# The inverse root of the norm of x: eight VectorE steps against one power on GpSimd

## The chip, the cores and the metric

The kernel runs on one core of a Trainium2 chip. Its time is the device time of one execution in microseconds (us). Five engines take part, each with an instruction queue of its own that it works off in order: TensorE (PE, with PEld for its weight loads), VectorE (DVE), ScalarE (ACT), GpSimd (POOL) and SyncE (SP, which here issues most of the transfers). An engine waits for another by a semaphore, and whatever stands behind a waiting instruction in the same queue waits with it.

## The reference, cut to what matters

Two blocks follow each other on 256 tokens of width 1024: a mixer block of two layers with a mixture of experts in each, and one attention block. Every stage begins with the same root-mean-square norm of x:

```python
def rms_norm(x, gain):
    xf = x.astype(jnp.float32)
    y = xf * lax.rsqrt(jnp.mean(xf * xf, axis=-1, keepdims=True) + EPS)
    return (y * gain.astype(jnp.float32)).astype(x.dtype)

for l in range(DEPTH):                      # DEPTH = 2
    h = rms_norm(x, attn_norm[l])
    proj = h @ w_in[l]
    ...                                     # matrix LSTM, attention, spatial gating
    x = x + y @ w_out[l]
    x = x + hier_moe(rms_norm(x, ffn_norm[l]), ...)
...
h = rms_norm_2(x, norm_w[l])                # the second block, once
proj = h @ w_in_2
```

That makes five norms of x: two at a mixer, two at a router of the experts, one at the second block. What the change touches is the `rsqrt` in these five, for 256 tokens, which lie as 128 partitions by 2 columns.

## The kernel before, in words

The 256 tokens are two tiles of 128 rows. The projections stream weights of 1 MB (`w`, five buffers, issued by SP in `pump`, line 188), and each chunk is split into two parts of reduced precision, `whi` by ScalarE (line 263) and `wlo` by VectorE (line 264). Every product is then three matmuls (lines 452, 453, 454) over eight slices of 128 channels. The experts' weights stream in the same way, unsplit.

The norm isn't applied to x before the product. `transpose_x` transposes the raw x, TensorE starts on the product at once, and the factor `rx` (one number for each token) comes in afterwards. `norm` (line 408) forms it: line 411 adds the two half sums of squares and EPS, and `rsqrt` (lines 334 to 341) takes an integer guess and eight VectorE steps to the inverse root. Who needs `rx`:

- In a mixer, `rh` (lines 504 and 505, VectorE) and `across` (line 426): TensorE spreads `rx` over the partitions with small matmuls, VectorE copies the result to `rb` (line 429). `across` stands in TensorE's queue amid the matmuls of the first projection.
- In a router, the scaled logits `lg` (line 953, VectorE). They head a chain of some twenty small VectorE steps up to `ab` (line 975), which TensorE needs for its next real work (line 977). Ahead of that it does 22 matmuls that serve nothing but to keep it busy (`warm(22)`, line 392).
- In the second block, `across` alone, and later the scales of the projections.

GpSimd does little: the rotary tables times a gain (lines 520 and 521, sixteen short products in each layer, from the table `row`, whose transfer line 291 issues), the mask of `wst` (line 698), `rg` (line 701) and some fills. In layer 1 `row` is loaded from ScalarE's queue when the layer begins.

The order on each engine is not the order of the source. The framework that builds the program sets it ahead of time from estimates of its own, and the engines then keep to it.

Of the kernel before, what the change touches and what calls it, by code (L numbers as in the profile page):

```python
# [15 lines left out]
OP = mybir.AluOpType  # L16
# [91 lines left out]
def block_kernel(ctx: ExitStack, tc: tile.TileContext, A, out):  # L108
    nc = tc.nc
# [41 lines left out]
    def small(shape, dt=F32, name="t", bufs=1):  # L151
        return sp.tile(shape, dt, name=name, tag=shared.get(name, name), bufs=bufs)
# [174 lines left out]
    def rsqrt(v):  # L327

        n = v.shape[1]
        c = (3.0 / 8) ** 0.2
        y, t = small([128, 24], name="rs_y", bufs=2)[:, :n], small([128, 24], name="rs_t", bufs=2)[:, :n]
        nc.vector.tensor_scalar(y.bitcast(I32), v.bitcast(I32), -0.5, 1597463007.0, op0=OP.mult, op1=OP.add)
        nc.vector.scalar_tensor_tensor(t, y, -0.5 * c, y, op0=OP.mult, op1=OP.mult)
        nc.vector.tensor_mul(t, t, v)
        nc.vector.scalar_tensor_tensor(y, t, 1.5 * c, y, op0=OP.add, op1=OP.mult)
        nc.vector.tensor_mul(t, y, y)
        nc.vector.tensor_mul(t, t, v)
        nc.vector.scalar_tensor_tensor(t, t, -2.251600503921509, t, op0=OP.add, op1=OP.mult)  # L340
        nc.vector.scalar_tensor_tensor(v, t, 2.2813665866851807, y, op0=OP.add, op1=OP.mult)
# [66 lines left out]
    def norm(s4):  # L408

        r = small([128, 2], name="rx", bufs=2)  # L410
        nc.vector.scalar_tensor_tensor(r, s4[:, :, 0], EPS, s4[:, :, 1], op0=OP.add, op1=OP.add)
        rsqrt(r)
        return r

    def norm_stats():
        s4 = small([128, 2, 2], name="ss4")
        for n in range(2):
            for j in range(2):
                square(s4, j, n)
        return norm(s4)  # L420
# [482 lines left out]
    class Router:  # L903
# [35 lines left out]
        def route(self):  # L939
            l, xh, xl, pt = self.l, self.xh, self.xl, self.pl  # L940
            R = row[l]
            warm(22)
            r = norm(self.s4)
            rh, r2 = small([128, 2], name="r_h"), small([128, 2], name="r_2")
            nc.gpsimd.tensor_scalar(rh, r, 0.5, None, op0=OP.mult)
# [727 lines left out]
```

## Time and profile before

| what | value |
|---|---|
| three timed runs | 964.05, 967.74, 968.22 us (median 967.74) |
| the profiled execution | 964.06 us, its span 962.3 us |
| TensorE busy (matmul) | 935.0 us, 97% of the span |
| TensorE weight loads | 617.4 us, 64% |
| VectorE busy | 473.9 us, 49% |
| ScalarE busy | 378.3 us, 39% |
| GpSimd busy | 18.3 us, 2% |
| HBM read | 271.27 MB, 285 GB/s over the span |

The 964.06 us of the profiled execution are 1.8 us more than its span, which runs from the first to the last instruction. The four executions stand at two levels, near 964 and near 968 us. TensorE is busy nearly throughout, and its busy time counts pipelined matmuls whose ends are modelled, so what matters are the places at which it waits. The layers begin near 5 and 374 us, their routers stand near 145 and 506 us, and the second block begins near 735 us.

### The profile page before, as it was taken

The numbers are of one execution on the slowest core, as the hardware profiler recorded it, in microseconds if no ns is written. First come the engines' busy times: TensorE is split into PE (matmuls) and PEld (weight loads), VectorE is DVE, ScalarE is ACT, GpSimd is POOL, SyncE is SP. The second block draws the span as 40 slices with busy tenths as digits, with TensorE's granted clock in tenths as the row PEclk, the third lists the DMA queues.
The fourth block names the chain that finished last, engine by engine and source line by source line (L and its number), as shares of the span: only waits on it lengthen the run. The fifth ranks groups of instructions, "written<-read, shape, count | busy, mean of one in ns | idle before, by whom it ended". The sixth has DMA issues, their size and how long they took to land. (4 is left out here: it accounts for less than half of the span.)

```text
span 962.3 us, 14955 instructions
## 1 busy us (share of the span) xinstructions
PE 935.0 (97%) x5818; PEld 617.4 (64%) x5818; DVE 473.9 (49%) x1131; ACT 378.3 (39%) x706; POOL 18.3 (2%) x60
## 2 busy tenths in 40 slices
PE   8989999999999998999999999999998999999998
PEld 6889884433344345889884433344345988899996
DVE  5698765221111225788665221111225777786574
ACT  5576542212122124485532212122124446745442
POOL 0100000000000001100000000000000000000000
PEclk8999999999999999999999999999999999999999
DMA  9537558899999998347558899999998542155531
GB/s 356 182 131 304 189 217 325 333 401 422 420 423 419 412 421 343 103 147 291 184 220 331 325 407 422 421 421 418 421 421 350 182 163 94 45 176 178 187 118 44
DMA packets 41436, 273.36 MB, mean 284 GB/s; under 512 B 5128, under 2 KB 7312, under 8 KB 9872
## 3 DMA queue, kind: packets, MB, share of 16 engines
q1 hardware_dynamic: 39008, 268.48, 71.0%
q10 hardware_dynamic: 2352, 3.87, 1.3%
q8 instruction: 48, 0.79, 0.3%
q14 instruction: 28, 0.23, 0.1%
HBM read 271.27 MB, written 2.63 MB: 285 GB/s over the span
## 5 line engine op out<-in xcount | busy, mean ns | idle before, releaser
L1128 PE MATMUL mm<-w,X 128*32 128x512 f32 (+1 forms) x1024 | 188.8, 598 | 1.8 <-DMA w<-in_w_e 1.8
L264 DVE TENSOR_TENSOR wlo<-w,whi 128x1024 fp32r<-128x1024 f32 (+3 forms) x124 | 145.2, 1182 | 26.8 <-ACT whi L263 26.7
L263 ACT ACTIVATE whi<-w 128x1024 fp32r<-128x1024 f32 (+3 forms) x124 | 122.5, 1017 | 76.4 <-issue 42.4
L1167 PE MATMUL mm<-w,ehT 128*32 128x512 f32 (+1 forms) x512 | 136.0, 600 | 3.9 <-DMA w<-in_w_e 1.5
L452 PE MATMUL mm<-hT,whi 128*128 128x256 f32 (+2 forms) x432 | 124.9, 290 | 0.2
L454 PE MATMUL mm<-hT,wlo 128*128 128x256 f32 (+2 forms) x432 | 124.1, 287 | 0.8 <-DVE wlo L264 0.8
L453 PE MATMUL mm<-lT,whi 128*128 128x256 f32 (+2 forms) x432 | 124.1, 288 | 0.0
L1128 PEld LDWEIGHTS mm<-w,X 128*32 128x32 f32 (+1 forms) x1024 | 47.8, 119 | 93.7 <-issue 83.0
L453 PE MATMUL mm<-wlo,hT 128*128 128x256 f32 x288 | 83.3, 289 | 1.1 <-DVE wlo L264 1.1
L452 PE MATMUL mm<-whi,hT 128*128 128x256 f32 x288 | 84.2, 292 | 0.0
L454 PE MATMUL mm<-whi,lT 128*128 128x256 f32 x288 | 83.2, 289 | 0.0
L452 PEld LDWEIGHTS mm<-hT,whi 128*128 128x128 f32 (+2 forms) x432 | 80.3, 186 | 2.3 <-issue 0.8
L453 PEld LDWEIGHTS mm<-lT,whi 128*128 128x128 f32 (+2 forms) x432 | 80.2, 186 | 1.8 <-issue 1.3
L454 PEld LDWEIGHTS mm<-hT,wlo 128*128 128x128 f32 (+2 forms) x432 | 80.2, 186 | 1.6 <-DVE wlo L264 1.3
L1115 ACT ACTIVATE X<-mm,vec 128x256 f32<-128x256 f32 (+1 forms) x96 | 43.4, 456 | 94.6 <-PE mm L1112 93.8
L1171 DVE TENSOR_TENSOR yhl<-mm,yhl 128x512 fp32r<-128x512 f32 x44 | 30.4, 692 | 95.2 <-ACT yhl L1170 93.2
L1167 PEld LDWEIGHTS mm<-w,ehT 128*32 128x32 f32 (+1 forms) x512 | 32.6, 119 | 68.2 <-issue 54.9
L1112 PEld LDWEIGHTS mm<-P,xh 128*128 128x128 f32 x192 | 29.2, 188 | 49.2 <-ACT X L1115 32.5
L1153 DVE TENSOR_SCALAR ePT<-mm,C 128x256 fp32r<-128x256 f32 x22 | 10.7, 484 | 100.4 <-ACT ehT L1151 100.4
L453 PEld LDWEIGHTS mm<-wlo,hT 128*128 128x128 f32 x288 | 55.0, 191 | 2.9 <-DVE wlo L264 1.5
L452 PEld LDWEIGHTS mm<-whi,hT 128*128 128x128 f32 x288 | 55.0, 191 | 1.4 <-issue 0.7
L454 PEld LDWEIGHTS mm<-whi,lT 128*128 128x128 f32 x288 | 55.0, 191 | 0.7 <-issue 0.2
(456 smaller groups left out, 1387.6 us busy)
## 6 DMA issues: line engine op xcount, KB each, us to landing
w<-in_w_e SPq DMA_DIRECT2D x192, 1024.0 KB, 13.2
w<-in_w_in SPq DMA_DIRECT2D x37, 1024.0 KB, 4.9
w<-in_w_out SPq DMA_DIRECT2D x12, 1024.0 KB, 4.9
w<-in_w_in SPq DMA_DIRECT2D x4, 768.0 KB, 5.3
w<-in_w_up_a SPq DMA_DIRECT2D x2, 1024.0 KB, 4.8
w<-in_w_up_b SPq DMA_DIRECT2D x2, 1024.0 KB, 4.8
w<-in_w_u SPq DMA_DIRECT2D x2, 960.0 KB, 12.2
w<-in_w_in SPq DMA_DIRECT2D x2, 800.0 KB, 13.2
```

Source lines behind the costliest of these rows:

```text
L263: nc.scalar.activation(hi[:, s_], w[:, s_], AF.Copy)
L264: nc.vector.tensor_sub(lo[:, s_], w[:, s_], hi[:, s_].bitcast(F32))
L452: nc.tensor.matmul(ps, st[0], mv[0], start=first, stop=False)
L453: nc.tensor.matmul(ps, st[0], mv[1], start=False, stop=False)
L454: nc.tensor.matmul(ps, st[1], mv[0], start=False, stop=last)
L1112: nc.tensor.matmul(ps[:, a, :n], t[:, j, k * 128:(k + 1) * 128], P[:, j], start=i == 0, stop=i == 3)
L1115: nc.scalar.activation(X[:, k, :n], ps[:, a, :n], AF.Identity, bias=0.0, scale=g[:, k:k + 1])
L1128: nc.tensor.matmul(ph[w * a:w * a + w], X[:, k, c0:c0 + w], take(kk_[a][k // 4])[:, (k % 4) * 512:(k % 4 + 1) * 512], start=k == 0, stop=k ...
L1153: nc.vector.tensor_scalar(PT, pT[:, 256:], cc("place" if w == 64 else "place32"), None, op0=OP.is_equal)
L1167: nc.tensor.matmul(py[w * a:w * a + w], hT[:, c * 128 + w * a:c * 128 + w * a + w], take(kk_[a][2])[:, c * 1024 + n * 512:c * 1024 + (n + ...
L1171: nc.vector.tensor_sub(yhl[:, n, 1], py, yhl[:, n, 0].bitcast(F32))
```

## The change

`norm` gets its inverse root from one GpSimd instruction: a tile of two columns is filled with -0.5, and `r` is raised to it. The fill is GpSimd's too. The tile carries the name `skr`, and so shares its single buffer with the mixer's `skr` of line 596. The other uses of `rsqrt` stay as they were.

```diff
     def norm(s4):
 
         r = small([128, 2], name="rx", bufs=2)
+        mhalf = small([128, 2], name="skr")
+        nc.gpsimd.memset(mhalf, -0.5)
         nc.vector.scalar_tensor_tensor(r, s4[:, :, 0], EPS, s4[:, :, 1], op0=OP.add, op1=OP.add)
-        rsqrt(r)
+        nc.gpsimd.tensor_tensor(r, r, mhalf, op=OP.pow)
         return r
```

With the source, the order that the framework sets changes too. Lines from 411 on have a number higher by two in the changed kernel.

GpSimd's queue where layer 1 begins, before (`cos_kr` and `sin_kr` are the last of sixteen products of the rotary tables with `row`):

```order
L1259 UNCONDITIONAL_BRANCH
L520 TENSOR_TENSOR cos_qr_3799<-cosT_111,row_3730 128x16
L521 TENSOR_TENSOR sin_qr_3800<-sinT_110,row_3730 128x16
...
L521 TENSOR_TENSOR sin_kr_3810<-sinT_110,row_3730 128x16
L698 TENSOR_TENSOR wst_4206<-wst_4206,C_69 128x512
L701 TENSOR_SCALAR rg_4209<-rx_3779 128x2
L759 MEMSET b8_4600 4x256
```

The same place in the changed kernel (`skr` is the tile of -0.5, line 414 the power):

```order
L1261 UNCONDITIONAL_BRANCH
L412 MEMSET skr_3766 128x2
L522 TENSOR_TENSOR cos_qr_3778<-cosT_111,row_3716 128x16
L523 TENSOR_TENSOR sin_qr_3779<-sinT_110,row_3716 128x16
...
L523 TENSOR_TENSOR sin_kr_3789<-sinT_110,row_3716 128x16
L414 TENSOR_TENSOR rx_3765<-rx_3765,skr_3766 128x2
L703 TENSOR_SCALAR rg_4188<-rx_3765 128x2
L700 TENSOR_TENSOR wst_4185<-wst_4185,C_69 128x512
L761 MEMSET b8_4579 4x256
```

The power stands behind all sixteen table products. In layer 0 it stands ahead of them, and of everything else but its fill.

TensorE's queue at `across` of layer 1, before (`hT`, `lT` are the transposed x, `whi_3177` and `wlo_3178` the layer's first chunk of weights):

```order
L452 MATMUL mm_3828<-hT_3732,whi_3177 128x256
L453 MATMUL mm_3828<-lT_3733,whi_3177 128x256
L454 MATMUL mm_3828<-hT_3732,wlo_3178 128x256
L426 MATMUL mm_3794<-C_69,rx_3779 128x128 x2
L454 MATMUL mm_3889<-hT_3732,wlo_3821 128x256
L452 MATMUL mm_3889<-hT_3732,whi_3820 128x256
```

And in the changed kernel (`mm_3807` is what `mm_3828` was):

```order
L455 MATMUL mm_3807<-lT_3719,whi_3163 128x256
L456 MATMUL mm_3807<-hT_3718,wlo_3164 128x256
L428 MATMUL mm_3773<-C_69,rx_3765 128x128 x2
L454 MATMUL mm_3807<-hT_3718,whi_3163 128x256
L455 MATMUL mm_3807<-lT_3719,whi_3163 128x256
L456 MATMUL mm_3807<-hT_3718,wlo_3164 128x256
```

`across` has moved up by 18 matmuls, into the first chunk's product. It moves up by 28 matmuls in layer 0 and by 10 in the second block.

VectorE's queue at the router of layer 0, before (`xl` is the low part of x, `lg` the scaled logits):

```order
L411 SCALAR_TENSOR_TENSOR rx<-ss_1369 128x2
L334 TENSOR_SCALAR rs_y<-rx 128x2
L335 SCALAR_TENSOR_TENSOR rs_t<-rs_y 128x2
L336 TENSOR_TENSOR rs_t<-rs_t,rx 128x2
L337 SCALAR_TENSOR_TENSOR rs_y<-rs_t,rs_y 128x2
L338 TENSOR_TENSOR rs_t<-rs_y 128x2
L339 TENSOR_TENSOR rs_t<-rs_t,rx 128x2
L937 TENSOR_TENSOR xl<-x,xh 128x512
L340 SCALAR_TENSOR_TENSOR rs_t<-rs_t 128x2
L341 SCALAR_TENSOR_TENSOR rx<-rs_t,rs_y 128x2
L953 TENSOR_TENSOR lg<-mm,rx 128x72
```

And in the changed kernel:

```order
L413 SCALAR_TENSOR_TENSOR rx<-ss_1362 128x2
L939 TENSOR_TENSOR xl<-x,xh 128x512
L955 TENSOR_TENSOR lg<-mm,rx 128x72
L956 TENSOR_TENSOR lb<-lg,row 128x72
L1016 TENSOR_REDUCE gm<-lg 128x2
```

Only the eight steps are gone there. A little further on, a step of the gates (line 1024) has moved ahead of `slot` (line 984). SP's queue is the same in both.

## Rows read from the trace of the kernel before

**Rows 1.** The page's totals: busy time, share of the span, instructions.

```profile
PE 935.0 (97%) x5818; PEld 617.4 (64%) x5818; DVE 473.9 (49%) x1131; ACT 378.3 (39%) x706; POOL 18.3 (2%) x60
```

**Rows 2.** Groups on GpSimd: form, count | busy us, mean ns | idle before.

```profile
L698 POOL TENSOR_TENSOR wst<-wst,C 128x512 f32<-128x512 f32 x2 | 3.7, 1838 | 4.7 <-DMA C<-in_consts 4.7
...
L946 POOL TENSOR_TENSOR r<-r_h,rx 128x2 f32<-128x2 f32 x2 | 0.5, 268 | 0.2
```

**Rows 3.** Timeline of layer 0's start: start us, duration us, engine, line.

```profile
13.59 0.16 DVE L411 SCALAR_TENSOR_TENSOR rx<-ss 128x2 f32<-128x2 f32 x1 [0.33 <-ACT junk L405]
...
15.64 0.28 PE L453 MATMUL mm<-lT,whi 128*128 128x256 f32 x1
```

**Rows 4.** Timeline of the second block's start.

```profile
741.17 0.16 DVE L411 SCALAR_TENSOR_TENSOR rx<-ss 128x2 f32<-128x2 f32 x1 [1.29 <-ACT junk L405]
...
742.74 0.16 DVE L341 SCALAR_TENSOR_TENSOR rx<-rs_t,rs_y 128x2 f32<-128x2 f32 x1
...
743.05 0.68 PE L426 MATMUL mm<-C,rx 128*128 128x128 f32 x4 [0.38 <-DVE rx L341]
```

**Rows 5.** Timeline of TensorE alone there.

```profile
742.27 0.28 PE L454 MATMUL mm<-whi,lT 128*128 128x256 f32 x1
742.39 0.28 PE L452 MATMUL mm<-whi,hT 128*128 128x256 f32 x1
```

**Rows 6.** Timeline of layer 0's router.

```profile
144.91 0.16 DVE L411 SCALAR_TENSOR_TENSOR rx<-ss 128x2 f32<-128x2 f32 x1 [0.25 <-ACT junk L405]
...
145.30 0.62 ACT L936 ACTIVATE xh<-x 128x512 fp32r<-128x512 f32 x1
...
146.17 0.69 DVE L937 TENSOR_TENSOR xl<-x,xh 128x512 fp32r<-128x512 f32 x1
146.37 4.10 PE L392 MATMUL mm<-ones_bf 128*128 128x512 bf16 x18
...
147.22 0.23 DVE L953 TENSOR_TENSOR lg<-mm,rx 128x72 f32<-128x72 f32 x1
...
150.76 0.19 PE L977 MATMUL mm<-ab,bf_lt 128*128 128x32 bf16 x1 [0.29 <-DVE ab L975]
```

**Rows 7.** TensorE's waits over the whole span: total us, times, longest.

```profile
PE mm L1194 <- DVE slot L984: 1.2, 2, 0.6
...
PE mm L426 <- DVE rx L341: 0.7, 2, 0.4
```

**Rows 8.** Timeline of layer 1's start, TensorE, VectorE, ScalarE and GpSimd.

```profile
372.86 0.34 ACTq L291 DMA_DIRECT2D row<-in_row  x1
...
380.25 0.15 DVE L411 SCALAR_TENSOR_TENSOR rx<-ss 128x2 f32<-128x2 f32 x1
380.65 0.22 POOL L520 TENSOR_TENSOR cos_qr<-cosT,row 128x16 f32<-128x16 f32 x1 [232.38 <-DMA row<-in_row]
380.77 1.23 DVE L264 TENSOR_TENSOR wlo<-w,whi 128x1024 fp32r<-128x1024 f32 x1 [0.37 <-ACT whi L263]
380.83 1.25 POOL L521 TENSOR_TENSOR sin_qr<-sinT,row 128x16 f32<-128x16 f32 x1
...
382.98 0.28 PE L454 MATMUL mm<-hT,wlo 128*128 128x256 f32 x1
383.62 0.68 PE L426 MATMUL mm<-C,rx 128*128 128x128 f32 x4 [0.36 <-DVE rx L341]
...
384.62 1.30 POOL L698 TENSOR_TENSOR wst<-wst,C 128x512 f32<-128x512 f32 x1
```

**Rows 9.** Stretches of the start: length, PE, PEld, DVE, ACT, POOL busy, clock, DMA.

```profile
7.00:8.00 1.00, 0.28 (x2) 0.20 (x2) 0.81 (x3) 1.00 (x4) 0.00 (x0) 0.98 1.07 430
8.00:9.00 1.00, 1.00 (x6) 0.72 (x5) 1.00 (x4) 0.98 (x3) 0.00 (x0) 0.50 1.16 471
```

**Rows 10.** Timeline of two matmuls at the lower clock.

```profile
13.76 0.41 PE L453 MATMUL mm<-lT,whi 128*128 128x256 f32 x1
...
13.97 0.41 PE L454 MATMUL mm<-hT,wlo 128*128 128x256 f32 x1
```

## The prediction

> **What bounds the kernel now.** The page's totals come first [rows 1]: TensorE is busy for 97% of the span and VectorE for 49%. Eight VectorE steps taken away are therefore worth nothing by themselves. What counts is whether TensorE, at one of the five places where a norm is formed, starts later or sooner. So the second view is the table of TensorE's waits [rows 7]. Two of its lines have to do with the norms: `across` waits for the last step of `rsqrt`, 0.7 us in two places, and the transposes of `slot` wait 1.2 us in two. A third is in the timeline of the router, 0.29 us at line 977 [rows 6]. These waits, 2.2 us in all, are the most that could come back directly. The rest of the reading is the timelines of the five places, TensorE beside VectorE and GpSimd, and GpSimd's queue beside them, since the power joins it.
>
> **The cost of one power.** Before has no power on GpSimd. The nearest row is a product of the same shape, two operands of 128x2, at 0.27 us. The longest group there, 128x512, takes 1.84 us [rows 2]. I take T = 0.5 us: the shape is that of the product, and a power is more arithmetic for each element. 0.27 and 1.84 stay as ends. The Trainium skill (GPSIMD Engine Reference, "Performance versus the Vector engine") has GpSimd about half as fast as VectorE in two-operand elementwise work, and no word on powers. By that rule an estimate would be 0.3 us, twice a VectorE step of 0.16 us, and the sum below would be 0.4 us less. A hop from one engine to the next costs about 0.15 us: `rsqrt` ends at 742.74 + 0.16 = 742.90, and `across` starts at 743.05 [rows 4]. The fill of -0.5 stands in GpSimd's queue well ahead of each power and costs nothing.
>
> **Layer 0's mixer.** The statistic is there at 13.59 + 0.16 = 13.75, the power runs from 13.90 to 13.90 + T, and TensorE could start `across` at 14.05 + T. In its new place `across` follows the matmul of 15.64 [rows 3], so TensorE gets there at 15.76. With T = 0.5 it is 1.2 us early: nothing lost. VectorE stands still meanwhile, in front of `rh` and then `rb`, with four `wlo` halves behind it. They are for the next chunk, and TensorE reaches that some 3 us later than `across`, so TensorE's own matmuls hide this. If T passed 1.7 us the cover would be gone. Counted at 0.
>
> **The two routers.** In layer 0 the statistic ends at 144.91 + 0.16 = 145.07, and the logits `lg` started at 147.22 [rows 6]. In the changed queue only `xl` lies between. It needs `xh`, which ends at 145.92, so it can run from about 146.0 to 146.7, and `lg` follows at 146.6: 0.6 us sooner. The power is done by 145.07 + 0.15 + T = 145.7, ahead of `xl`. TensorE cannot collect all of this, since its 18 filler matmuls run to 146.37 + 4.10 = 150.47 whatever VectorE does. It gets the 0.29 us of line 977. In layer 1 the same gain can only show at `slot`, where 0.6 us are waited [rows 7]; I take 0.3 us there too. Sum -0.6 us, with ends 0 and -1.2.
>
> **Layer 1's mixer, the term that decides.** Here the power stands in GpSimd's queue behind the sixteen table products, and the first of these waits for the transfer of `row`, issued at 372.86 and landed just ahead of 380.65 [rows 8]. The products ended when `wst` began, at 384.62. So the power, though its input is there at 380.40, runs from 384.62 to 384.62 + T, and `across` can start at 384.77 + T = 385.27. In before the eight VectorE steps had the factor ready for a start at 383.62. That alone would be 1.65 us. But `across` has also moved up by 18 matmuls. TensorE used to reach it at 382.98 + 0.12 = 383.10, at the full-clock spacing of 0.12 us [rows 5], and now reaches it at 383.10 - 18 x 0.12 = 380.94. It then stands from 380.94 to 385.27, which is 4.33 us, where it stood for 0.52 us. The 18 matmuls that used to fill this time are queued behind `across`. Loss 3.8 us (3.3 + T). VectorE stands in front of `rh` from 382.0 on, with the split of a later chunk behind it; TensorE reaches that chunk only after more than 50 further matmuls, so this hides.
>
> **The clock after that stall.** At the start of the kernel TensorE has little to do while x comes in (0.28 us busy in the slice from 7 to 8), and the granted clock falls from 0.98 to 0.50 of full speed, to the level of 1.2 GHz [rows 9]. It is still low at 13.97, where matmuls stand 0.21 us apart [rows 10], though TensorE has been busy for most of the time since 8.0; at 15.64 a matmul lasts 0.28 us again instead of 0.41 [rows 3]. I take it that 4.3 us without a matmul bring the same fall. Each us of work at the low level loses 1 - 0.12/0.21 = 0.43 us. If the level stays low as long as at the start, some 6 us, and part of that lies in the stall itself, the loss is about 2.0 us; the ends are 0 (no fall) and 6 x 0.43 = 2.6. The Trainium skill (TensorE: The Clock Gate, "The HAM clock gate") calls the low clock the default state, which activity releases; by that rule the fall is certain and the sum 5.5 us. The rows show one fall, after a stretch with some work in it; without a fall the sum is 3.5.
>
> **The second block.** The statistic ends at 741.33, the power at 741.48 + T, and `across` can start at 741.63 + T = 742.13. TensorE reached it at 742.39 + 0.12 = 742.51 [rows 5] and waited to 743.05, 0.54 us. Ten matmuls earlier it arrives at 741.31 and waits 0.82 us: +0.3 us (T - 0.22).
>
> **Sum.** 0 - 0.6 + 3.8 + 2.0 + 0.3 = +5.5 us. The low end (T 0.27, no fall, routers -1.2) is 3.6 + 0 - 1.2 = +2.4; the high end (T 1.84, 2.6 for the clock, routers 0, layer 0 +0.1) is 5.1 + 2.6 + 1.6 + 0.1 = +9.4. Against the profiled execution's 964.06 us the sum gives 969.6. The median of the three runs is 967.74, and they lie at two levels, 964 and 968, which I cannot tell apart by cause. Counted from the median the sum gives 973.2. I take the middle, 971.5 us.
>
> **The rivals.**
> - *The clock holds.* A fall was seen only at the start, and no later wait of TensorE in the trace is near 4 us, so none tests it. Then 3.5 us remain: 967.6 to 971.2, or 969.5.
> - *The power is long.* Nothing in the trace measures it. Each us of T beyond 0.5 costs 1 us in layer 1 and 1 in the second block. Beyond 1.7 us it also costs 1 in layer 0, and soon as much at each router, where fillers cover only part. T = 3 would mean 2.5 + 2.5 + 1.3 + 2 x 1 = 8.3 us more: 980.
> - *`row` comes early enough, and nothing is lost.* Everything in layer 1 hangs on the landing of one small transfer at 380.5, 7.6 us after its issue. The sixteen products take 4 us from there, with 1.0 us of this because `sin_qr` (1.25 us, next to 0.22 us for its neighbour) stands still while `wlo` runs on VectorE [rows 8]. If `row` landed by about 376.5, GpSimd's queue would be empty when the statistic comes at 380.40. The factor would be there at 380.55 + T = 381.05, and `across`, started at 381.2, would wait 0.26 us instead of 0.52. Then the total is -0.3 + 0.3 - 0.6 = -0.6 us, and the kernel is not slower: 963.5 to 967.1. For this speaks that a small table need not take that long. Against it speaks that the weights fill the DMA engines just then, and that the change does nothing to the order of the transfers.
>
> **How the numbers follow.** Half a per cent, 4.8 us, is about what a measurement of this kernel tells from no change. The forecast (the queue wait and the fall) has 0.53; its own range is +3.8 to +8 us, and some 0.34 of it lies above 4.8. The clock holds: 0.2, nearly all within half a per cent. The long power: 0.13, slower. `row` early: 0.08, within. What I haven't thought of: 0.06, shared out. Faster 0.04, same 0.43, slower 0.53. The range of 966 to 977 takes in the first two cases at both levels of the base and the beginning of the third; what lies outside is mostly the long power and the early `row`.
>
> **What would show it.** Right, if in the changed profile the power of layer 1 starts just behind the last `sin_kr`, about 4 us after its input; if TensorE's longest wait is at `across` (line 428) there, above 4 us; and if the granted clock falls below 1 in the slices behind it. The router's `lg` should come about 0.6 us sooner than before, counted from line 411 (now 413). Wrong, if the power's own row is over 1 us, if the clock stays at 1.0 after the stall, if TensorE waits less than 2 us at that `across`, or if layer 0 or the routers show a wait for `rx` that is not there now.

## The result and the profile after

The changed kernel takes 971.07 us (median of 8 runs, 969.07 to 973.2), the kernel before 965.31 us in the same comparison (8 runs, 963.1 to 968.22). The ratio is 1.006, with a 95% interval of 1.0042 to 1.0078: slower by 5.8 us. The prediction was +5.5 us, 971.5 us. The profiled execution of the changed kernel took 972.61 us, its span 970.8 us.

The totals of the page after, which answer to [rows 1]: VectorE has lost forty instructions and 7 us of work, and GpSimd has gained 3 us.

```profile
PE 940.9 (97%) x5818; PEld 622.5 (64%) x5818; DVE 466.7 (48%) x1091; ACT 378.0 (39%) x706; POOL 21.3 (2%) x70
```

TensorE's waits after, to be read against [rows 7] (total us, times, longest):

```profile
PE mm L428 <- POOL rx L414: 4.8, 2, 4.0
...
PE mm L1196 <- DVE slot L986: 0.9, 2, 0.5
```

The wait at `slot` went from 1.2 to 0.9 us, and the wait at line 977 (now 979) is gone from the table. The wait at `across` went from 0.7 to 4.8 us, and 4.0 us of it is a single wait. It stands in layer 1. The timeline of that place, answering to [rows 8] (start us, duration us, engine, line):

```profile
382.72 0.15 DVE L413 SCALAR_TENSOR_TENSOR rx<-ss 128x2 f32<-128x2 f32 x1
...
382.95 0.22 POOL L522 TENSOR_TENSOR cos_qr<-cosT,row 128x16 f32<-128x16 f32 x1 [226.10 <-DVE rx L413]
...
383.25 1.22 DVE L264 TENSOR_TENSOR wlo<-w,whi 128x1024 fp32r<-128x1024 f32 x1 [0.37 <-ACT whi L263]
383.29 0.28 PE L456 MATMUL mm<-hT,wlo 128*128 128x256 f32 x1
383.31 1.24 POOL L522 TENSOR_TENSOR cos_qr<-cosT,row 128x16 f32<-128x16 f32 x1
...
386.66 0.22 POOL L523 TENSOR_TENSOR sin_kr<-sinT,row 128x16 f32<-128x16 f32 x1
386.84 0.72 POOL L414 TENSOR_TENSOR rx<-rx,skr 128x2 f32<-128x2 f32 x1
387.59 0.17 DVE L506 TENSOR_SCALAR rh<-rx 128x2 f32<-128x2 f32 x1 [3.12 <-POOL rx L414]
...
387.61 1.22 PE L428 MATMUL mm<-C,rx 128*128 128x128 f32 x4 [4.05 <-POOL rx L414]
```

The input of the power is ready at 382.87. The power starts at 386.84, behind the last table product, and takes 0.72 us. TensorE's last matmul ahead of `across` starts at 383.29, so the next could have started at 383.41; `across` starts at 387.61. That is 4.20 us without a matmul. The row of 382.95 names the norm's line as what released the first product, but releasers are inferred: the transfer of `row` was issued at 375.3 and landed 7.5 us later, at 382.8, and in version 7 below the first product starts at 382.92, ahead of the norm's line at 383.50. The products wait for `row`, as in before.

The clock in the stretches around it (length, busy time of PE, PEld, DVE, ACT and POOL, granted clock, DMA):

```profile
382.00:384.00 2.00, 1.56 (x14) 1.36 (x12) 1.63 (x5) 1.21 (x3) 1.05 (x3) 1.00 0.34 127
384.00:386.00 2.00, 0.00 (x0) 0.00 (x0) 0.47 (x1) 0.00 (x0) 2.00 (x10) 0.88 0.36 43
386.00:388.00 2.00, 0.39 (x2) 0.39 (x3) 0.25 (x2) 0.00 (x0) 1.91 (x8) 0.50 0.87 344
388.00:390.00 2.00, 2.00 (x11) 2.00 (x11) 0.42 (x1) 0.00 (x0) 1.41 (x2) 0.50 0.02 6
390.00:392.00 2.00, 2.00 (x11) 2.00 (x11) 0.00 (x0) 0.00 (x0) 0.00 (x0) 0.50 0.00 0
392.00:394.00 2.00, 2.00 (x18) 2.00 (x17) 0.41 (x1) 1.50 (x3) 0.00 (x0) 0.92 0.00 0
```

The clock is at its upper level (2.4 GHz) until the stall, falls in the middle of it to 0.50 (1.2 GHz), and stays there for more than 4 us after work has begun again: 11 matmuls in 2 us instead of 18.

**Where the time went, segment by segment.** The norm's first line (L411 before, L413 after) appears once in each part of the program, so its five starts cut a profile into segments that can be compared one by one. In before it starts at 144.91, 380.25 and 741.17 [rows 4, 6, 8] and, in layer 1's router, at 505.83; in after at 147.59, 382.72, 514.11 and 749.34. Differences of these, in us, the last segment up to the end of the span:

| profile | start to router 0 | router 0 to layer 1 | layer 1 to router 1 | router 1 to second block | second block to the end |
|---|---|---|---|---|---|
| before | 144.91 | 235.34 | 125.58 | 235.34 | 221.13 |
| after | 147.59 | 235.13 | 131.39 | 235.23 | 221.46 |
| difference | +2.68 | -0.21 | **+5.81** | -0.11 | +0.33 |

The 5.81 us of the third segment match the 5.8 us between the medians. The first one is no work of the power: it varies from 143.6 to 147.6 us in the table below, with the length of the low clock, and is 144.59 us in version 1, with the power in layer 0, and 147.54 in version 2, without it. Two rows from after's start, TensorE's timeline:

```profile
16.44 0.41 PE L454 MATMUL mm<-hT,whi 128*128 128x256 f32 x1
...
16.87 0.61 PE L428 MATMUL mm<-C,rx 128*128 128x128 f32 x4
```

In this execution matmuls still take the 0.41 us of the lower level at 16.44, where those of before had been back at 0.28 by 15.64 [rows 3], and `across` of layer 0 waits for nothing. (The stretches of after show a granted clock of 1.00 here; the durations say otherwise, and I go by them.) And from 96 to 98 us, far from any norm, after has a fall to 0.50 that before's profile lacks. Other executions show it too, the one with the power in layer 1 alone (below) for longest.

The second block, after, answering to [rows 4]:

```profile
749.34 0.16 DVE L413 SCALAR_TENSOR_TENSOR rx<-ss 128x2 f32<-128x2 f32 x1 [1.29 <-ACT junk L405]
749.64 0.72 POOL L414 TENSOR_TENSOR rx<-rx,skr 128x2 f32<-128x2 f32 x1 [226.56 <-DVE rx L413]
...
750.42 0.71 PE L428 MATMUL mm<-C,rx 128*128 128x128 f32 x4 [0.78 <-POOL rx L414]
```

And layer 0's router, answering to [rows 6]:

```profile
147.91 0.72 POOL L414 TENSOR_TENSOR rx<-rx,skr 128x2 f32<-128x2 f32 x1 [38.06 <-DVE rx L413]
...
148.64 0.69 DVE L939 TENSOR_TENSOR xl<-x,xh 128x512 fp32r<-128x512 f32 x1 [0.88 <-ACT xh L938]
...
149.33 0.23 DVE L955 TENSOR_TENSOR lg<-mm,rx 128x72 f32<-128x72 f32 x1
```

`lg` comes 149.33 - 147.59 = 1.74 us after the norm's line, and came 147.22 - 144.91 = 2.31 us after it: 0.57 us sooner. What TensorE gets of it shows at the transposes of `slot`, before first and after second, the router of layer 0 and that of layer 1:

```profile
151.63 0.39 PE L1194 MATMUL mm<-C,slot 128*32 128x128 f32 x2 [0.58 <-DVE slot L984]
...
512.29 0.39 PE L1194 MATMUL mm<-C,slot 128*32 128x128 f32 x2 [0.58 <-DVE slot L984]
```

```profile
153.73 0.39 PE L1196 MATMUL mm<-C,slot 128*32 128x128 f32 x2 [0.46 <-DVE slot L986]
...
520.26 0.39 PE L1196 MATMUL mm<-C,slot 128*32 128x128 f32 x2 [0.47 <-DVE slot L986]
```

Counted from the norm's line of the same router they start 6.72 and 6.46 us later in before, 6.14 and 6.15 us later in after.

### The profile page after: what moved, and what is told of

Read it like the earlier page. It is cut to its first block, busy times and chain, and to the rows that moved or that the text cites. A ratio compares the mean times of both kernels' runs of the same rounds, so it can differ in the third digit from the quotient of the medians.

```text
span 970.8 us, 14932 instructions
## 1 busy us (share of the span) xinstructions
PE 940.9 (97%) x5818; PEld 622.5 (64%) x5818; DVE 466.7 (48%) x1091; ACT 378.0 (39%) x706; POOL 21.3 (2%) x70
```

## The experiments

The theory: all of the loss is in layer 1's mixer, in two parts. `across` waits for a power that is queued behind sixteen table products (3.7 us), and the wait lets the clock fall (2.1 us). The rivals: the power's own length costs, wherever it stands; or the low clock would come there anyway; or the late factor delays VectorE. Each run's time is set beside runs of the kernel before on the same chip; the ratio with its 95% interval is worked out over all of these runs and is not the quotient of the two medians. First the segments of all profiles, worked out as above; a version is named by its section below.

| profile | start to router 0 | router 0 to layer 1 | layer 1 to router 1 | router 1 to second block | second block to the end |
|---|---|---|---|---|---|
| 1, layer 1 by VectorE | 144.59 | 235.58 | 125.56 | 235.24 | 221.53 |
| 2, layer 1 alone | 147.54 | 235.42 | 131.88 | 235.21 | 221.05 |
| 3, power first | 143.64 | 236.86 | 125.47 | 240.53 | 221.50 |
| 4, across behind the first chunk | 143.64 | 235.42 | 128.62 | 235.35 | 221.47 |
| 5, early fillers | 144.72 | 236.14 | 131.41 | 239.34 | 221.49 |
| 6, fillers in the wait | 145.00 | 236.24 | 127.84 | 235.35 | 221.47 |
| 7, across late | 147.60 | 235.90 | 126.46 | 235.24 | 221.50 |
| 8, across late twice | 144.77 | 235.97 | 126.47 | 235.22 | 220.47 |
| 9, first and late | 143.58 | 235.73 | 125.47 | 234.78 | 220.54 |

**1. Layer 1's mixer back on VectorE, the other norms by power.**

```
     def norm(s4, where=None):
         r = small([128, 2], name="rx", bufs=2)
+        if where == ("mixer", 1):
+            nc.vector.scalar_tensor_tensor(r, ...)
+            rsqrt(r)
+            return r
```

> Layer 1's mixer gets its eight VectorE steps back; the other four norms keep the power. Theory (the loss is made at layer 1's across: 4.2 us of waiting in place of 0.5, and about 2.1 us of low clock behind it): across of layer 1 waits about 0.4 us for VectorE, the clock stays at 1.0 there, and the kernel is within 1 us of before (about -0.2: routers -0.5, second block +0.25), some 5.8 us under the changed kernel. Rival (the loss is spread over all five powers): only about a fifth of the 5.8 us comes back, so it stays 4 us or more above before.

Measured: 965.31 us, before 964.88; ratio 1.0012 (0.9988 to 1.0035). The loss is gone. TensorE at layer 1's `across`:

```profile
382.88 0.28 PE L460 MATMUL mm<-hT,wlo 128*128 128x256 f32 x1
383.54 0.68 PE L432 MATMUL mm<-C,rx 128*128 128x128 f32 x4 [0.38 <-DVE rx L341]
```

The wait is before's again, and the layer-1 segment is 125.56 us, before's 125.58.

**2. The power in layer 1's mixer alone**, the condition of 1 turned round (`where != ("mixer", 1)`).

> The power only in the norm ahead of layer 1's mixer; the four other norms as before. Theory (the loss is all there, the other places give back 0.3 to 0.6 us each at the routers and take 0.2 at the second block): slower than before by about 5.8 us (970.7), a little slower than the changed kernel itself; wait of the across near 4 us, clock 0.50 for about 5 us behind it. Rival (a part of the loss comes from the other places, such as the longer low clock at the start or the fall at 95 to 99 us of the changed kernel's profile): slower by 3 us or less.

Measured: 970.16 us, before 965.24; ratio 1.0038 (1.001 to 1.0065). The interval, 1.0 to 6.3 us, doesn't say how much of the loss this one power makes. The profile does:

```profile
387.85 1.01 PE L432 MATMUL mm<-C,rx 128*128 128x128 f32 x3 [4.05 <-POOL rx L418]
```

Its layer-1 segment is 6.3 us longer than before's, with the same wait as in the changed kernel. (The clock fell later in this stall and rose later behind it: granted 1.00 from 384 to 386 and 0.57 from 392 to 394, against 0.88 and 0.92 in after.) Without the power there the loss is gone (1), with it alone the loss is there: the place is settled.

**3. Power first.** The table products are made to read a value worked out from the power's result (times zero, added to their factor), so that GpSimd must do the power ahead of them. `across` stays where the change put it.

```
+        if l:
+            z = small([128, 2], name="rg")
+            nc.gpsimd.tensor_scalar(z, r, 0.0, None, op0=OP.mult)
+            nc.gpsimd.tensor_tensor(R[:, :64], R[:, :64], z[:, 0:1].to_broadcast([128, 64]), op=OP.add)
```

> In layer 1 the table products are made to depend on the power (a zero made from its result is added to their table), so the power stands ahead of them in GpSimd's queue; across stays moved up. Two small GpSimd instructions more. Theory (the power waits for the products in its own queue): the power starts within 0.2 us of its statistic. If it gets through before the wlo half on VectorE, across waits about 0.7 us and the kernel is within 1 us of before. If the wlo half holds it, as it held one product for 1.0 us, the factor comes about 1.6 us after the statistic and across waits 1.5 us: about +1 us. Rival (the power is slow after a long pause of GpSimd, whatever stands ahead): it takes well over 0.7 us even here, and the loss stays near +5.8 us.

Measured: 965.12 us, before 964.88; ratio 0.9997 (0.9981 to 1.0014). Two more GpSimd instructions, and the loss is gone. The start of layer 1:

```profile
380.50 0.15 DVE L413 SCALAR_TENSOR_TENSOR rx<-ss 128x2 f32<-128x2 f32 x1
...
380.79 0.72 POOL L414 TENSOR_TENSOR rx<-rx,skr 128x2 f32<-128x2 f32 x1 [227.89 <-DVE rx L413]
...
381.03 1.23 DVE L264 TENSOR_TENSOR wlo<-w,whi 128x1024 fp32r<-128x1024 f32 x1 [0.38 <-ACT whi L263]
...
381.57 0.60 PE L428 MATMUL mm<-C,rx 128*128 128x128 f32 x3 [0.22 <-POOL rx L414]
```

The power takes the same 0.72 us, and TensorE waits 0.22 us for it, though `across` stands eighteen matmuls earlier in the queue than in before. So neither the length of the power nor the place of `across` costs anything alone: it is the queue in front of the power. (The 240.53 us of this profile's fourth segment hold one wait of 5.7 us of TensorE's own sequencer ahead of the second block, not seen elsewhere, with the clock at 0.50 behind it; this execution is the longest of the twelve.)

**4. `across` behind the first chunk's product**, about where it stood before, the power queued as in the change.

```
-        rb = across(r)
+        if l == 0:
+            rb = across(r)
 ...
         chan(pq, hT, w0, 0, 128)
+        if l:
+            rb = across(r)
```

> The power and its place in GpSimd's queue as in the changed kernel; across of layer 1 is written after the first chunk's product, which puts it back where it stood before, 18 matmuls later. Theory: TensorE arrives 2.2 us later, so it waits about 2.0 us in place of 4.2, and with so short a wait the clock holds: +1.6 us for layer 1, about +1.4 us against before in all. Rival (the queue wait alone makes the loss, wherever across stands): +5.8 us as in the changed kernel. If the wait is 2.0 us and the clock falls all the same: about +3.5 us.

Measured: 967.78 us, before 964.88; ratio 1.002 (1.0001 to 1.004). The wait is less than half of the changed kernel's, and the clock falls even so, where I expected it to hold. TensorE, and two stretches:

```profile
383.94 0.71 PE L428 MATMUL mm<-C,rx 128*128 128x128 f32 x4 [1.88 <-POOL rx L414]
...
387.65 0.41 PE L456 MATMUL mm<-hT,wlo 128*128 128x256 f32 x1
387.87 0.32 PE L454 MATMUL mm<-hT,whi 128*128 128x256 f32 x1
```

```profile
382.00:384.00 2.00, 0.12 (x2) 0.06 (x1) 0.08 (x2) 2.00 (x4) 1.91 (x9) 1.00 0.81 295
384.00:386.00 2.00, 2.00 (x12) 2.00 (x13) 1.48 (x4) 1.20 (x2) 1.75 (x3) 0.63 0.16 65
```

The layer-1 segment is 3.04 us longer than before's: some 1.5 us more wait than before's 0.36, and the rest, 1.5 us, by matmuls that stand 0.21 us apart until 387.87. A wait half as long still paid most of the clock's price.

**5. Early fillers:** twenty dummy products ahead of layer 1's `across`, to keep TensorE busy through the wait.

```
+        if l == 1:
+            warm(20)
         rb = across(r)
```

> Twenty filler matmuls stand ahead of across of layer 1, about 4.3 us at full clock, so that TensorE is busy while it would wait; their results are used by nothing. Theory (some 2.1 us of the loss are the clock): across starts as late after the statistic as in the changed kernel, but the clock stays at 1.0 behind it, and the kernel comes out about 2 us under the changed one, +3.7 us against before. Rival (the clock's share is small, the wait is all): no difference to the changed kernel, +5.8 us.

Measured: 973.9 us (6 runs), before 964.88; ratio 1.0071 (1.0048 to 1.0093). This doesn't test what it was meant to. The scheduler placed fillers and `across` nineteen matmuls earlier still, and the fillers need nothing, so they ran before the wait and not in it. TensorE:

```profile
379.27 4.55 PE L392 MATMUL mm<-ones_bf 128*128 128x512 bf16 x20
385.59 0.71 PE L428 MATMUL mm<-C,rx 128*128 128x128 f32 x4 [1.77 <-POOL rx L414]
```

```profile
386.00:388.00 2.00, 2.00 (x19) 2.00 (x18) 0.42 (x1) 0.00 (x0) 1.42 (x2) 1.00 0.10 40
```

The clock stayed at 1.00, behind the wait of 1.77 us too, where one of 1.88 us was followed by a fall in 4. But fillers and wait together take 4.55 + 1.77 = 6.3 us of TensorE's time from the layer, about as much as stall and low clock did (4.20 + 2.1), and the layer-1 segment is that of the changed kernel, 131.41 us. A filler that takes the place of work saves nothing. That this version is slower by another 3 us lies, in its profile, in the fourth segment (239.34 us): TensorE waits there 2.5 us for weights at 578, where the longest such wait in before's segment is 0.6 us, and the clock is low behind it (0.63 from 579 to 582). What brings this wait on I have not followed.

**6. Fillers in the wait.** The same idea, with twelve fillers that can start only once the norm's sum is there: their operand is written again (1.0, from the sum times zero plus one) ahead of the power.

```
+        if fill:
+            nc.vector.tensor_scalar(ones_bf, r[:, 0:1], 0.0, 1.0, op0=OP.mult, op1=OP.add)
+            ps = mm("b")
+            for _ in range(fill):
+                nc.tensor.matmul(ps, ones_bf.to_broadcast([128, 128]), ones_bf.to_broadcast([128, 512]), ...)
         nc.gpsimd.tensor_tensor(r, r, mhalf, op=OP.pow)
```

> Layer 1 alone: 12 dummy matmuls that can start only once the sum of squares is written stand ahead of the across, which comes nine rows later in TensorE's order than in the changed kernel (row 1668 against 1659, fillers not counted). In the changed kernel the first chunk lands (first cx) 17.53 us after L413, against 11.70 in the kernel before: some 3.7 us of it the wait and 2.1 us the low clock. Theory that the low clock is a price of its own, brought on by TensorE standing still: with the fillers the clock stays at 1.00 in 385 to 393, the across starts as long after L413 as in the changed kernel (4.9 us), nine products more (9 x 0.12 = 1.1 us) are done by then, and cx lands 17.5 - 2.1 - 1.1 = 14.3 us after L413; against the kernel before about +2.5 us (967.5). Theory that the low clock comes on its own there, whatever TensorE does meanwhile: the clock falls even so, and cx lands about 16.4 us after L413 (+4.7 us, 969.6).

Measured: 967.35 us, before 965.24; ratio 1.0013 (0.9988 to 1.0039). TensorE and one stretch:

```profile
382.89 0.28 PE L461 MATMUL mm<-hT,wlo 128*128 128x256 f32 x1
383.12 2.79 PE L418 MATMUL mm<-ones_bf 128*128 128x512 bf16 x11
385.78 0.71 PE L433 MATMUL mm<-C,rx 128*128 128x128 f32 x4
```

```profile
384.00:386.00 2.00, 2.00 (x11) 0.92 (x10) 0.24 (x2) 0.00 (x0) 1.91 (x8) 1.00 0.87 280
```

The power is as late as in the change (it starts 3.8 us after the norm's line, there 4.1), TensorE does useless work instead of none, and the clock stays at 1.00. The first chunk's `cx` comes 395.23 - 381.24 = 13.99 us after the norm's line; in the changed kernel it was 17.53, in before 391.95 - 380.25 = 11.70. Of the 3.54 us between this version and the change, nine matmuls that run ahead of the fillers make 1.1 and the power that is done sooner after the norm's line 0.35; 2.1 us are left for the clock. So the low clock would not have come here on its own: it came where TensorE stood still, and has a price of its own.

**7. `across` behind the second chunk's product**, just ahead of the one product that reads it; the power stays late.

```
+        if l:
+            rb = across(r)
         nc.vector.tensor_mul(cx[:, 0], pk[:, 1], rb)
```

> The power everywhere as changed, but layer 1's across is written behind the second chunk's product (TensorE row 1723 against 1659), just ahead of the one product that reads it. Theory (what costs is only that TensorE's next product stands behind the across): no wait of the across in layer 1, clock 1.00 from 380 to 400, cx 11.7 us after L413 or less, and the time that of the kernel before less the routers' gain, 0.3 to 0.9 us below it (964 to 964.6), which is hardly to be told from no change. Rival (the late power itself costs, by VectorE's rh that waits 3.1 us for it or by rb): slower than before by 1 us or more.

Measured: 966.6 us, before 965.24; ratio 1.0005 (0.9975 to 1.0036). No wait at `across` and no fall of the clock there. VectorE's `rh` still waits 2.2 us for the power, and the first `cx` comes 394.17 - 383.50 = 10.67 us after the norm's line, 1.03 us sooner than in before. So a late power costs nothing where `across` comes late enough to find it done: the loss takes both, the queue ahead of the power and the early `across`.

But the layer-1 segment is 126.46 us, 0.88 us longer than before's, and the expected gain of 0.3 to 0.9 us is not there. The reason lies 50 us behind the norm. TensorE waits there for ScalarE's `P`, in before and in 7:

```profile
429.82 0.70 PE L661 MATMUL mm<-kT,qT 96*128 96x256 f32 x2 [1.52 <-ACT P L655]
...
433.13 0.70 PE L666 MATMUL mm<-kT,qT 96*128 96x256 f32 x2 [1.73 <-ACT P L660]
```

And the stretches behind these waits, before first:

```profile
430.00:432.00 2.00, 2.00 (x17) 1.86 (x18) 1.32 (x4) 2.00 (x7) 0.00 (x0) 1.00 0.60 135
...
434.00:436.00 2.00, 2.00 (x11) 2.00 (x11) 1.91 (x5) 0.95 (x4) 0.00 (x0) 0.50 0.50 123
```

This wait is 0.21 us longer than in before, and the clock, which holds at 1.00 there, falls. (That the 0.21 us bring the fall is not shown.) From the matmul behind the wait to the first one of the next kind (433.73 in before, 438.09 here) pass 4.96 us with 15 matmuls of the projection in them, where before takes 3.91 us with 19; with the four at 0.12 us each that is 1.5 us lost. 1.5 + 0.2 - 1.0 are 0.7 of the 0.88 us. The next version shows the same wait (1.73 us), the same fall and the same 0.89 us.

**8. The same, and the second block's `across` behind its first projections** (sixteen matmul rows later).

```
 def second():
-        rb = across(r)
-        rb2 = bc(rb, 1, 2)
 ...
         qa = normed(0, 0)
+        rb = across(r)
+        rb2 = bc(rb, 1, 2)
```

> As the run with the across behind the second chunk, and the second block's across also written behind its first projections (TensorE row 3268 against 3252). Theory: its wait of 0.78 us (0.38 before) goes too, so 0.4 us or so less than the kernel before from there and 0.3 to 0.9 from the routers: 963.5 to 964.5, the lowest of all versions. Rival (the reader of rb is then late by as much): no change against the run with one across moved.

Measured: 964.6 us, before 965.24; ratio 0.9985 (0.9961 to 1.0009). The last segment is 220.47 us: 0.66 us less than before's and 1.0 less than the change's. The change's wait of 0.78 us is gone, and nothing else has taken its place.

**9. Power first in layer 1 (3), and the second block's `across` late (from 8).**

> The version in which layer 1's table products wait for the power (so that the power runs first on GpSimd), with the second block's across written behind its first projections besides. Theory: layer 1 as in the kernel before (wait of the across 0.2 us, clock 1.00, 134.4 us from the last block's final products to the router's norm), the second block 0.7 us shorter than before (220.5 us from its norm's L413 to the end, as in the run with both across moved), the routers 0.2 to 0.6 less: 0.9 to 1.4 us below the kernel before, the lowest of all versions. Rival (something that every version with the power shares, such as memsets or queues on GpSimd, costs about as much as the routers give): no more than 0.5 us below the kernel before.

Measured: 962.92 us, before 965.25; ratio 0.9982 (0.9956 to 1.0007). The lowest median of all versions, and each of its segments behind the first two is below before's. The interval takes in no change. Two short waits are left at `across`, in total us, times, longest:

```profile
PE mm L428 <- POOL rx L414: 0.7, 2, 0.4
```

One is layer 1's 0.22 us, the other 0.43 us at layer 0: in this execution the start ran at the full clock, and TensorE reached layer 0's `across` before the power was done. The profiles of 3, 4 and 6, whose start ran at the full clock too, show 0.44 to 0.45 us there.

## Why the prediction was right, step by step

- **Where the loss is: right.** Layer 1's mixer has all of it (experiments 1 and 2), by the queue in front of the power (3) together with an `across` that stands too early to find it done (7). The rival of an early `row` is out: it landed 7.5 us after its issue, as in before (7.6). No run brings it sooner, so what that would save is not measured.
- **The stall: right.** 4.33 us were predicted, 4.20 measured. TensorE came to `across` 383.41 - 382.72 = 0.69 us after the norm's line, as worked out (380.94 - 380.25 = 0.69). The power was longer than T, and the products began and ended 0.2 us sooner after the norm's line than in before; the errors cancel, which is luck.
- **T: too low, 0.72 instead of 0.5 us.** The five powers took 0.70 to 0.73 us. The product of the same shape that I leaned on was no good neighbour, and the estimate by the Trainium skill's ratio between the engines, 0.3 us (GPSIMD Engine Reference, "Performance versus the Vector engine"), was further off: the rows of this case put the power at more than twice that. It mattered little, since the queue cost five times as much as the power.
- **The clock: right in sign and size.** Predicted 2.0 us. In after the low level costs about 0.4 us at `across` (0.87 us to the next matmul, 0.44 in version 1) and some 1.7 us in the nineteen or so matmuls up to 392.54, 2.1 us in all; experiment 6 gives 2.1 us by another way. 3.7 + 2.1 are the 5.81 us of the segment. I had drawn the fall from one at the kernel's start and given it the same length. Experiments 4, 7 and 8 show that a wait less than half as long can bring it, 5 that it need not. The rule that I cited from the Trainium skill (TensorE: Matmul & The Clock Gate, "The HAM clock gate": the low clock is the default, which activity releases) agrees with 6, where matmuls without use kept the upper level. That it makes a fall certain was too much to draw from it: behind the 1.77 us of 5 there is none.
- **The routers: the gain is there and then lost from sight.** Predicted -0.6 us. The transposes of `slot` come 0.58 us sooner in layer 0 and 0.31 in layer 1, 0.9 us together, but over their whole segments only 0.21 and 0.11 us are left. Even these can't be told from nothing: version 2, whose routers have no power, has 235.42 and 235.21 us there, and the versions whose routers have it lie at 235.13 to 236.86 and, but for the long waits of 3 and 5, at 234.78 to 235.35. Later in these segments TensorE waits for weights, and I take it that what it gained ahead of such a wait it gives back there; no run tests this. With 0.3 us for this term the sum would be the 5.8 us of the medians, but the interval of the result, 4.1 to 7.5 us, doesn't resolve such differences, and that forecast and medians lie 0.3 us apart is in part luck.
- **The second block: right.** +0.3 predicted, +0.33 measured; its wait is 0.78 us, worked out as 0.82.
- **Layer 0: right in these profiles, by the cover that was named.** TensorE gets to `across` after the power. Profiles 3, 4, 6 and 9 show the condition that I hadn't seen: this holds only when the start runs at the low clock; otherwise 0.43 to 0.45 us are waited. The row of 15.64 from which I worked out the cover is one of a start at the low clock.
- **The base.** I took the middle between two levels of the kernel before, which is 0.7 us above the median of the eight runs; that 971.5 lies so near 971.07 is in part luck too, since the sum is short by 0.3 us. The profiles show one thing that moves a whole execution by 2 to 4 us: how long the clock is low at the start, and whether it falls again near 96 us. A single profiled time of this kernel is no better than that. The layer-1 segment and the last one lie within 0.1 us of each other in versions with the same code there, with one exception (131.39 us in after, 131.88 in experiment 2, where the clock rose later).

## What to carry to other kernels

Before a step goes to an idle engine, read what is queued ahead of it on that engine at the moment when its input is ready: here the engine was 2% busy, and the sixteen small products that cost nothing where they stood made the step 4 us late. Taking instructions off one engine can also change the order on another: with the power in layer 1 (the change, 2 and 3) `across` stood 18 matmuls earlier than without it (before and 1), and held up work that used to fill the time. Price a TensorE stall with the low clock that can follow it, look for that clock in the whole profile and not only at the place that was changed (7), and put the step first in its queue or its reader last in its own, rather than fill the gap.

## What the runs showed of the hardware that was not expected

- A power over 128x2 on GpSimd takes 0.69 to 0.73 us in all profiles, also with work on VectorE beside it: the one of 380.79 ran next to a `wlo` of 1.23 us at no loss (experiment 3), where a small product next to a `wlo` took 1.24 us instead of 0.22 (383.31 in after). The GpSimd instruction just behind that power, over 128x2 as well, took 0.77 us; the one behind the power in after, of the same form, took 0.23 us.
- A wait of 1.88 us was followed by the lower clock (experiment 4), at a place where TensorE had been busy without a gap before, and so were waits of 1.73 us (7 and 8). One of 1.77 us (5) and one of 1.52 us (before, at `P`) were not. So the length of the wait alone doesn't decide it; what else does stays open.
- The granted clock fell at about 95 us in the profiles of some versions and not in those of others, though the code there is the same and TensorE was as busy just ahead: 0.91 us from 92 to 94 in the profile of experiment 2, with the fall, and in that of experiment 8, without it. What decides between them stays open.
